# The last two tiles' products of v and gates are dealt out between the last group's maxima, and the first head's row goes ahead of v

## The chip, the cores and the metric

The kernel runs on one core of a Trainium2 chip. The metric is the device time of one execution in microseconds (us); several executions are timed and their median is compared. One execution is also taken by the hardware profiler; it has a time of its own.

The engines are named as in the profile: PE is the matrix engine (PEld its weight loads), DVE the vector engine, ACT the scalar engine, POOL the general engine, SP the engine that issues most DMAs. A name with q behind it (SPq, ACTq) is the DMA queue that the engine feeds.

## The reference, cut to what matters

One layer over a sequence of 2048 tokens with width 1024. The input projection gives q, k and v (8 heads of 64) and u and g (512 columns each):

```
proj = einsum('bsd,de->bse', rms_norm(x), w_in)       # 1024 -> 3*512 + 2*512
q, k = per-head rms_norm(q), rms_norm(k)
a    = dilated_attention(q, k, v)     # branches (window, dilation) = (128,1), (512,4), (2048,16)
m    = spatial_gating(gelu(u), gelu(g), ...)
x    = x + concat(rms_norm(a), rms_norm(m)) @ w_out
x    = x + square(relu(rms_norm(x) @ w_ff1)) @ w_ff2
```

Each branch is a causal window softmax over the keys with the same residue, and the three branches are added with the weights of their softmax denominators. The kernel needs one number for each query and head that is at least as large as any of its scores, so that the exponentials don't overflow; it takes the largest score over the three branches. All products are done in a 32-bit form in which a number is held as a high and a low part: a product is three matmuls (high by high, low by high, high by low).

## The kernel before, in words

**Sweep 1** (`sweep1`, L340 to L613) goes over 16 tiles of 128 tokens. For each tile t it projects q, k and v (columns c = 0, 1, 2), 24 matmuls of 128x512 each (`gemm3`; 8 blocks of the width by three products). q and k are normed; v is split and stored (`v_d`, one store a tile, L572). Behind the product of the next tile, `behind(t, q, k, step)` does the rest of a tile in three steps: step 0 transposes q and k, splits them and stores them (`qt_d`, `kt_d`); step 1 (`max1`) computes the scores of the first branch again and takes their maxima; step 2 folds these into the tile's row of maxima. After every four tiles (a group G) the maxima of the second branch follow (`max4`), dealt out as `late4` over the next four tiles; `fold4` merges them and `store_m` stores the row to `mx_d`.

A call of `maxima` takes the units two by two, called a *pair* here: two matmuls into one bank `ps_sc` (L452) and two DVE maxima that read them (L456). There are two such banks. `max1` has four pairs for a tile (operand `qz`, 128 rows). `max4` has two pairs for a head and group (operand `qhi`, 64 rows, every fourth element of `kring` and `qhi`), 16 pairs for the 8 heads.

At the end of sweep 1 there is no next tile to stand between: `behind(15, 0)`, then the gates' products g of tiles 14 and 15 (24 matmuls each; their weights are loaded and split from t = 15 on into the places of q's weights: DMA `graw`, ACT `zh`, DVE `zl`), then `behind(15, 1)` (four pairs), `behind(15, 2)`, and `rest`, the second branch's maxima of the last group. Each g is copied by ACT into one buffer `ge` (L589) and stored to `ge_d` (ACT queue, L590).

**Attention** (`attention`, from L616) goes over the 8 heads. `prepare(h)` issues the loads on SP: `qh` (high part of q, loaded twice, once into rows 0 to 63 and once into rows 64 to 127), `ks` (high and low part of k), `q2` (low part of q) and `k2` (high part of k), and on the ACT queue `m14`, the stored maxima (L646). `load_v(1)` loads v for the first branch (`v1`), `load_v(4)` those for the two others. The maxima of the third branch are taken here: `group(r0)` (L662) does four matmuls `ps_mx<-ks,qh`; after four groups, DVE merges the result with `m14`, PE transposes it, and DVE's `nm` (minus the maximum) is sent by a DMA, here called the *row*, into row 64 of `q2`, so that the score matmul subtracts it by itself. The row has to be there before the second score matmul of the head can run.

For a head there are 20 jobs of scores, exponentials and products with v (`ps_as` L74, then `ps_o`): jobs 0 to 7 for the first branch, then four times two jobs for the second branch and one for the third. The groups of the next head are laid at the jobs named in `MXAT`. For head 0 there is no head before it, so sweep 1's last pairs are put around its groups: the pairs of heads 0 and 1 before `attention`, those of heads 2 and 3 ahead of its groups, those of heads 4 to 7 behind the row.

**What sets the order.** A scheduler places the instructions of an engine, except those given by `InOrder` or by a name in `en.pinned`: these stay in program order on their engine. All of attention is in order on every engine (its lines read L74 in the profile, the line of the helper). DMA issues of SP and of ACT are in order within their engine, and an issue waits for the data it sends, for its buffer, and for the DMA that had its completion counter before it.

Of the kernel before, what the change touches and what calls it, by code (L numbers as in the profile page):

```python
# [8 lines left out]
F32 = mybir.dt.float32  # L9
F32R = mybir.dt.float32r  # L10
AF = mybir.ActivationFunctionType
# [5 lines left out]
P = 128  # L17
S = 2048
D = 1024
H = 8  # L20
HD = 64
AW = H * HD
GW = 512
# [3 lines left out]
NT = S // P  # L27
KD = D // P
VW = 2 * HD + 2
# [5 lines left out]

MXAT = (5, 8, 11, 14)
V1AT, V4AT = 12, 4
# [10 lines left out]
LATE_H = 4  # L48
RH = 4
SPL = 0  # L50
LAB = True
WP1 = ()
BYP = ((0, 0),)
# [6 lines left out]
PIN2, PINM, PINE = 12, (), ()  # L60
PSB, MXB, HS0 = 4, 1, 0


# [40 lines left out]
def tile_hybrid_block(  # L104
# [20 lines left out]
    nc = tc.nc  # L125
# [180 lines left out]
    wg = {}  # L306
# [33 lines left out]
    def sweep1():  # L340
        if True:
# [7 lines left out]
            zh, zl = wg_tiles()  # L349
            wh = [zh] + [[wp.tile([P, AW], F32R, name=f"wh{c}_{k}") for k in range(KD)] for c in (1, 2)]  # L350
            wl = [zl] + [[wp.tile([P, AW], F32R, name=f"wl{c}_{k}") for k in range(KD)] for c in (1, 2)]
            vts = []
# [54 lines left out]
            def transposed(qn, gain, hi, lo):  # L407
                pt = pst.tile([P, 4, P], F32, tag="tr", name="ps_tr")
                for j in range(4):
                    nc.tensor.transpose(pt[:, j, :], qn[:, j * P : (j + 1) * P], ident)  # L410
# [33 lines left out]

            order = [nc.tensor, nc.vector]

            def maxima(m, units):

                for i in range(0, len(units), 2):
                    ps = pss.tile([P, 2, 256], F32, tag="sc", name="ps_sc")  # L450
                    for j, (qv, kv, mk, col) in enumerate(units[i : i + 2]):
                        order[0].matmul(ps[:, j, : mk.shape[1]], qv, kv, start=True, stop=True)  # L452
                    for j, (qv, kv, mk, col) in enumerate(units[i : i + 2]):
                        n = mk.shape[1]
                        jk = sp.tile([P, 256], F32, tag="jk", name="jk", bufs=1)
                        order[1].tensor_tensor_reduce(  # L456
                            jk[:, :n], ps[:, j, :n], mk, 1.0, -3e38, ALU.add, ALU.max, accum_out=m[:, col : col + 1]
                        )
# [84 lines left out]
            def late4(t, n):  # L543
# [6 lines left out]
                if tg == 3:  # L550
                    fold4(G, m4s.pop(G))
                    store_m(G, range(H))

            last = None
            gsrc = w_in[:, 3 * AW + GW : 3 * AW + 2 * GW]
            for t in range(NT):
                en.pinned = PINT if t < 1 else ()
                if 0 < t < NT - 1:
                    xs[t + 1] = load_x_t(xp, pst, t + 1, newton=True)
                _, xh, xl, r = xs[t]  # L560
                ns = []
                for c in range(3):
                    ps = psm.tile([P, AW], F32, tag="mm", name="ps_mm")
                    gemm3(ps, [(xh[:, k, :], xl[:, k, :], wh[c][k], wl[c][k]) for k in range(KD)], (t, c) in BYP)
                    if (t, c) == (0, X1AT):
                        xs[1] = load_x_t(xp, pst, 1, newton=True, xt=x_1)
                    if c < 2:
                        ns.append(normed(ps, r))
                    else:
                        vt = vts[t % 2]  # L570
                        split_sb(vt[:, :, 0:HD], vt[:, :, HD + 2 : VW], ps.rearrange("p (h d) -> p h d", d=HD), r)
                        nc.sync.dma_start(v_d[:, t * P : (t + 1) * P, :].rearrange("h t c -> t h c"), f32(vt))  # L572
                    if last is not None:
# [8 lines left out]
                late4(t, 2)  # L582
            behind(NT - 1, *last, 0)
            for t in (NT - 2, NT - 1):
                _, xh, xl, r = xs[t]
                ps = psm.tile([P, AW], F32, tag="mm", name="ps_mm")
                gemm3(ps, [(xh[:, k, :], xl[:, k, :], wg["h"][k], wg["l"][k]) for k in range(KD)])
                ge = sp.tile([P, GW], F32, tag="sq", name="ge", bufs=1)
                nc.scalar.activation(ge, ps, AF.Copy, scale=r)  # L589
                nc.scalar.dma_start(ge_d[t - NT + 2], ge)  # L590
            behind(NT - 1, *last, 1)
            behind(NT - 1, *last, 2)
            G = NT // 4 - 1
            nc.vector.memset(m4s[G], -3e38)

            def rest(heads):
                max4(G, m4s[G], qhis[G], heads)
                fold4(G, m4s[G])
                store_m(G, heads)

            rest(range(0, 2))
            st.close()
# [13 lines left out]
    def attention(finish, xnp, xs, tpe, wu):  # L616
        with ExitStack() as st:
# [12 lines left out]
            def prepare(h):  # L630
# [30 lines left out]

                def group(r0, psm=psm, queue=sy):  # L662
                    ps = psm.tile([P, 4, P], F32, tag="mx", name="ps_mx")
                    for j in range(4):
                        s = r0 + j
                        pe.matmul(ps[:, j, :], qh[0:HD, s * P : (s + 1) * P], ks[0:HD, s::16], start=True, stop=True)

                    def row():
                        nm = tp.tile([P, P], F32R, tag="nm", name="nm", bufs=1)[:16]
                        dve.tensor_scalar(nm, ps[:16, 0, :], -1.0, None, ALU.mult)  # L670
                        queue.dma_start(f32(q2[HD : HD + 1, :]), f32(nm))

# [826 lines left out]
```

## Time and profile before

| | us |
|---|---|
| timed executions | 2424.43, 2413.07, 2421.35 |
| their median | 2421.35 |
| the profiled execution's own time | 2430.62 |
| its span | 2428.9 |
| mean granted PE clock in it | 0.963 |
| sweep 1's last tiles to the first score of head 0 | about 330 to 410 in the span |
| attention | about 410 to 700 in the span |

A timeline row has the start in us from the span's start, the duration, the engine, the line, the operation with out<-in, the shape and count, and in brackets the idle time of the engine ahead of it and what ended it. Matmuls overlap in the pipe, so the distance of two starts is what one costs, not its duration. A row of windows has, for each stretch of time, the busy time and number of instructions of each engine, then the granted PE clock (1.00 is full, 0.50 half), the share of DMA time and the GB/s moved. The page's line of PE clock holds it in tenths for 40 slices of 60.7 us.

### The profile page before, as it was taken

The numbers are of one execution on the slowest core, as the hardware profiler recorded it, in microseconds if no ns is written. First come the engines' busy times: TensorE is split into PE (matmuls) and PEld (weight loads), VectorE is DVE, ScalarE is ACT, GpSimd is POOL, SyncE is SP. The second block draws the span as 40 slices with busy tenths as digits, with TensorE's granted clock in tenths as the row PEclk, the third lists the DMA queues.
The fourth block names the chain that finished last, engine by engine and source line by source line (L and its number), as shares of the span: only waits on it lengthen the run. The fifth ranks groups of instructions, "written<-read, shape, count | busy, mean of one in ns | idle before, by whom it ended". The sixth has DMA issues, their size and how long they took to land. (4 is left out here: it accounts for less than half of the span.)

```text
span 2428.9 us, 31778 instructions
## 1 busy us (share of the span) xinstructions
PE 2346.2 (97%) x11292; PEld 1962.2 (81%) x11292; DVE 1462.1 (60%) x2940; ACT 972.6 (40%) x1584; POOL 861.2 (35%) x691
## 2 busy tenths in 40 slices
PE   8999998999997999998989998999999999999999
PEld 7877776999995888777778886788878888888887
DVE  6666676556555656665875558655547565565542
ACT  5323323566663222223535555555543232222321
POOL 1101103555551222221566776677752001221210
PEclk9999997789888999998999999999999999999999
DMA  5445358576833333333666456655559665575652
GB/s 189 86 88 109 71 113 177 166 191 175 230 114 94 96 100 94 87 95 122 207 201 180 148 155 200 188 151 152 156 180 332 211 204 187 185 241 179 192 172 78
DMA packets 432302, 382.35 MB, mean 157 GB/s; under 512 B 89704, under 2 KB 358632, under 8 KB 427528
## 3 DMA queue, kind: packets, MB, share of 16 engines
q1 hardware_dynamic: 415408, 377.68, 53.4%
q10 hardware_dynamic: 16736, 2.65, 0.7%
q8 instruction: 89, 1.46, 0.2%
q14 instruction: 69, 0.57, 0.1%
HBM read 259.80 MB, written 120.39 MB: 157 GB/s over the span
## 5 line engine op out<-in xcount | busy, mean ns | idle before, releaser
L1298 PE MATMUL ps_f<-hop,wop 128*128 128x512 f32 x2688 | 620.3, 393 | 13.4 <-ACT hop L188 3.2
L1420 PE MATMUL ps_f<-split 128*128 128x512 f32 x2688 | 611.0, 390 | 2.8 <-ACT c L1285 2.8
L1298 PEld LDWEIGHTS ps_f<-hop,wop 128*128 128x128 f32 x2688 | 507.4, 189 | 124.6 <-ACT hop L188 5.0
L1420 PEld LDWEIGHTS ps_f<-split 128*128 128x128 f32 x2688 | 505.7, 188 | 108.0 <-ACT c L1285 3.2
L1210 POOL TENSOR_TENSOR as<-w1r 128x512 f32<-128x512 f32 x160 | 211.7, 1331 | 167.1 <-DVE wop L189 147.0
L1430 DVE TENSOR_TENSOR acc<-acc,ps_f 128x512 f32<-128x512 f32 x192 | 124.5, 683 | 212.1 <-PE ps_f L1420 212.0
L188 ACT ACTIVATE split<-sr 128x1024 fp32r<-128x1024 f32 x112 | 118.4, 1059 | 333.2 <-PE ps_f L1420 324.8
L1210 POOL TENSOR_TENSOR raw<-raw 128x1024 f32<-128x1024 f32 x40 | 101.0, 2532 | 420.8 <-DMA raw<-in_w_ff_dram 353.0
L1210 POOL TENSOR_TENSOR c<-c 128x512 f32<-128x512 f32 x160 | 233.5, 1482 | 45.8 <-ACT c L1286 45.8
L74 POOL TENSOR_TENSOR pl<-e,ph 128x512 fp32r<-128x512 f32 x144 | 175.2, 1229 | 145.4 <-ACT e L74 116.0
L189 DVE TENSOR_TENSOR wop<-as,wop 128x512 fp32r<-128x512 f32 x160 | 151.2, 945 | 88.3 <-ACT wop L188 85.6
L188 ACT ACTIVATE wop<-as 128x512 fp32r<-128x512 f32 x160 | 100.5, 629 | 210.6 <-POOL as L1210 122.4
L74 DVE TENSOR_TENSOR ps_as<-ps_as,mk 128x512 f32<-128x512 f32 (+1 forms) x160 | 105.9, 664 | 123.1 <-PE ps_as L74 112.7
L189 DVE TENSOR_TENSOR split<-sr,split 128x1024 fp32r<-128x1024 f32 x112 | 157.1, 1404 | 17.1 <-ACT split L188 12.5
L74 PE MATMUL ps_o<-ph,v 128*64 128x128 f32 (+3 forms) x816 | 154.2, 276 | 1.8 <-ACT nacc L74 1.4
L74 PE MATMUL ps_as<-qh,ks 128*128 128x256 f32 (+1 forms) x384 | 143.2, 378 | 0.0
L74 ACT ACTIVATE ph<-ps_as 128x512 fp32r<-128x512 f32 (+1 forms) x160 | 92.3, 577 | 125.3 <-DVE ps_as L74 125.0
L74 PE MATMUL ps_as<-q,k 65*128 65x256 f32 (+1 forms) x384 | 139.0, 371 | 0.0
L456 DVE CUSTOM_DVE_ANT_0 jk<-ps_sc,mk 128x256 f32<-128x256 f32 (+1 forms) x232 | 92.5, 399 | 45.8 <-PE ps_sc L452 39.7
L526 POOL CAST qz<-qhi 64x512 fp32r<-64x512 f32 x32 | 19.6, 613 | 274.4 <-ACT qhi L414 273.4
L74 PEld LDWEIGHTS ps_o<-ph,v 128*65 128x65 f32 (+1 forms) x816 | 114.7, 158 | 2.2 <-ACT nacc L74 1.6
L74 PEld LDWEIGHTS ps_as<-qh,ks 128*128 128x128 f32 x384 | 108.3, 282 | 2.9
(266 smaller groups left out, 4109.2 us busy)
## 6 DMA issues: line engine op xcount, KB each, us to landing
s_d<-c SPq DMA_DIRECT2D x224, 256.0 KB, 2.2
sr<-s_d SPq DMA_DIRECT2D x112, 512.0 KB, 3.6
raw<-in_w_ff_dram SPq DMA_DIRECT2D x96, 512.0 KB, 4.9
w1r<-in_w_ff_dram SPq DMA_DIRECT2D x128, 256.0 KB, 3.0
v<-v_d SPq DMA_DIRECT2D x24, 1040.0 KB, 12.3
xt<-in_x_dram SPq DMA_DIRECT2D x32, 512.0 KB, 4.0
raw<-h_d SPq DMA_DIRECT2D x28, 512.0 KB, 5.5
v_d<-vt SPq DMA_DIRECT2D x16, 520.0 KB, 7.9
```

The costliest lines, as they stand in the source:

```text
L74: return self.tc.keep_in_program_order(op(*args, **kwargs))
L188: en.scalar.activation(dst_hi, raw, AF.Copy)
L189: (en.gpsimd if on_pool else en.vector).tensor_tensor(dst_lo, raw, f32(dst_hi), ALU.subtract)
L456: order[1].tensor_tensor_reduce(jk[:, :n], ps[:, j, :n], mk, 1.0, -3e38, ALU.add, ALU.max, accum_out=m[:, col : col + 1])
L526: nc.gpsimd.tensor_copy(qz[rows, hh], f32(qhis[G][rows, :, cols]))
L1210: nc.gpsimd.tensor_tensor(dst, a, b, op)
L1298: nc.tensor.matmul(ps[bank], a[:, k, :], b[k], start=first and k == n == 0, stop=(k == 3 and n == 2), skip_group_check=True,)
L1420: nc.tensor.matmul(ps, s[a][:, k, :], t[b][:, k % 2, :], start=k == m == 0, stop=k == NH - 1 and m == 2)
L1430: nc.vector.tensor_tensor(c, c, ps, op)
```

## The change

The change has five parts.

1. The v products of tiles 14 and 15 and the g products of both, 96 matmuls, no longer stand in blocks. They become a list of *fillers*, taken one by one in order (v14, v15, g14, g15): 12 behind the k product of tile 15, 8 and 12 ahead of steps 0 and 1 of `behind(15)`, and 3 between the matmuls and the DVE maxima of each pair from then on. From tile 15's last step on, PE is pinned to this order.
2. All 16 pairs of the last group run in sweep 1 (heads 0 and 1, then 2 to 7), none around head 0's groups. `finish` only closes pools.
3. Head 0's row goes out on the SP queue like those of the other heads, and its `load_v(1)` is issued behind the row and no longer with the head's other loads.
4. `prepare` loads `qh` twice first and `ks` as one DMA of 128 rows; a group's matmul takes 128 rows (both parts of k) in place of 64.
5. `MXAT` is (7, 9, 12, 14) in place of (5, 8, 11, 14). The weights of v are allotted ahead of those of k.

```diff
-MXAT = (5, 8, 11, 14)
+MXAT = (7, 9, 12, 14)
+FILL, FILL0, FILL1, FILL2 = 3, 12, 8, 12
...
+            fillers = []
+            def fill(n):
+                for f in [fillers.pop(0) for _ in range(min(n, len(fillers)))]:
+                    f()
             def maxima(m, units):
...
                         order[0].matmul(ps[:, j, : mk.shape[1]], qv, kv, start=True, stop=True)
+                    fill(FILL)
                     for j, (qv, kv, mk, col) in enumerate(units[i : i + 2]):
...
+            def in_parts(t, w, store):
+                _, xh, xl, r = xs[t]
+                got = {}
+                def part(k, n):
+                    if k == n == 0:
+                        got["ps"] = psm.tile([P, AW], F32, tag="mm", name="ps_mm")
+                    a, b = ((xh, w[0]), (xh, w[1]), (xl, w[0]))[n]
+                    end = (k, n) == (KD - 1, 2)
+                    en.tensor.matmul(got["ps"], a[:, k, :], b[k], start=k == n == 0, stop=end)
+                    if end:
+                        store(t, got["ps"])
+                return [lambda k=k, n=n: part(k, n) for k in range(KD) for n in range(3)]
...
+                    elif t < NT - 2:
+                        store_v(t, project(t, c))
...
+                    if t == NT - 1 and c == 2:
+                        en.pinned, order[0] = ("tensor",), en.tensor
+                        for u in (NT - 2, NT - 1):
+                            fillers += in_parts(u, (wh[2], wl[2]), store_v)
+                        for u in (NT - 2, NT - 1):
+                            fillers += in_parts(u, (wg["h"], wg["l"]), store_g)
+                        fill(FILL0)
                     if last is not None:
                         behind(t - 1, *last, c)
...
-            behind(NT - 1, *last, 0)
-            for t in (NT - 2, NT - 1):
...
-                gemm3(ps, [(xh[:, k, :], xl[:, k, :], wg["h"][k], wg["l"][k]) for k in range(KD)])
...
-            behind(NT - 1, *last, 1)
-            behind(NT - 1, *last, 2)
+            for step in range(3):
+                fill((FILL1, FILL2, 0)[step])
+                behind(NT - 1, *last, step)
             G = NT // 4 - 1
             nc.vector.memset(m4s[G], -3e38)
-            def rest(heads):
+            for heads in (range(0, 2), range(2, H)):
                 max4(G, m4s[G], qhis[G], heads)
                 fold4(G, m4s[G])
                 store_m(G, heads)
-            rest(range(0, 2))
+            fill(len(fillers))
+            en.pinned = ()
             st.close()
             def finish(pe, dve):
-                order[:] = pe, dve
                 yield lambda pool: load_x_t(pool, pst, 0, nxt=1)
-                rest(range(2, RH))
                 yield
-                rest(range(RH, H))
                 late.close()
...
-                sy.dma_start(f32(qh[0:HD, :]), qt_d[h, 0:HD, :])
-                sy.dma_start(f32(ks[0:HD, :]), kt_d[h, 0:HD, :])
-                sy.dma_start(f32(ks[HD:P, :]), kt_d[h, HD:P, :])
+                for rows in (slice(0, HD), slice(HD, P)):
+                    sy.dma_start(f32(qh[rows, :]), qt_d[h, 0:HD, :])
+                sy.dma_start(f32(ks), kt_d[h])
                 sy.dma_start(f32(q2[0:HD, :]), qt_d[h, HD:P, :])
-                sy.dma_start(f32(qh[HD:P, :]), qt_d[h, 0:HD, :])
...
-                        pe.matmul(ps[:, j, :], qh[0:HD, s * P : (s + 1) * P], ks[0:HD, s::16], start=True, stop=True)
+                        pe.matmul(ps[:, j, :], qh[:, s * P : (s + 1) * P], ks[:, s::16], start=True, stop=True)
...
-                        queue.dma_start(f32(q2[HD : HD + 1, :]), f32(nm))
+                        sy.dma_start(f32(q2[HD : HD + 1, :]), f32(nm))
...
             T, group, load_v = prepare(0)
-            load_v(1)
...
-                for reduce in [group(r0, psx if r0 else psm, nc.scalar) for r0 in range(0, 16, 4)]:
+                for reduce in [group(r0, psx if r0 else psm) for r0 in range(0, 16, 4)]:
                     reduce()
                 due(True)
                 due(True)
+            load_v(1)
```

**PE at the end of sweep 1, before.** `zh` and `zl` are the gates' weights, `xh` and `xl` the tile, `kring` the keys, `ps_tr<-ident,m` the transposes of a fold. These rows run from the last g product to the first scores of head 0.

```order
L226 MATMUL ps_mm<-zl_3542,xh 128x512
L227 MATMUL ps_mm<-zh_3538,xl 128x512
L452 MATMUL ps_sc<-kring,qz 128x256 x8
L452 MATMUL ps_sc<-kring,qhi 128x256 x2
L478 MATMUL ps_tr<-ident,m_3818 8x128
L452 MATMUL ps_sc<-kring,qhi 128x256 x6
L500 MATMUL ps_tr<-ident,m_3850 8x128 x4
L74 MATMUL ps_sc<-kring,qhi 128x256 x8
L74 MATMUL ps_tr<-ident,m_3850 8x128 x4
L74 MATMUL ps_mx<-ks,qh 128x128 x16
L74 MATMUL ps_mx<-ident,m_3915 16x128
L74 MATMUL ps_sc<-kring,qhi 128x256 x16
```

The same place of the changed program, its last rows ahead of the first score:

```order
L458 MATMUL ps_sc<-kring,qhi 128x256 x2
L74 MATMUL ps_mm<-zh_3510,xl 128x512
L74 MATMUL ps_mm<-zh_3510,xh 128x512
L74 MATMUL ps_mm<-zl_3514,xh 128x512
L458 MATMUL ps_sc<-kring,qhi 128x256 x2
L74 MATMUL ps_mm<-zh_3510,xl 128x512
L458 MATMUL ps_sc<-kring,qhi 128x256 x4
L507 MATMUL ps_tr<-ident,m_3803 8x128 x4
L74 MATMUL ps_mx<-ks,qh 128x128 x16
L74 MATMUL ps_mx<-ident,m_4005 16x128
L74 MATMUL ps_as<-qh,ks 128x256
L74 MATMUL ps_as<-q_3995,k_3996 128x256
```

The 16 pairs of the last group (32 matmuls `ps_sc<-kring,qhi`) stood bare behind the products, 8 of them (16 matmuls) behind head 0's transpose. They now have three products behind each of the first 13 and one behind the 14th; two are bare, and between the transpose and the first score nothing is left.

**SP's queue for head 0, before**, from its first load on (`q_3904` and `k_3905` are q2 and k2, `v_3916` is v1; the loads of head 1 follow):

```order
L74 DMA qh<-qt_d 64x2048
L74 DMA ks<-kt_d 64x2048 x2
L74 DMA q_3904<-qt_d 64x2048
L74 DMA qh<-qt_d 64x2048
L74 DMA k_3905<-kt_d 64x2048
L74 DMA v_3916<-v_d 128x16x130
L74 DMA qh<-qt_d 64x2048
L74 DMA ks<-kt_d 64x2048 x2
```

And of the changed program, where `q_3995` and `k_3996` are q2 and k2, `v_4068` is v1:

```order
L571 DMA v_d<-vt_191 128x8x130
L74 DMA qh<-qt_d 64x2048 x2
L74 DMA ks<-kt_d 128x2048
L74 DMA q_3995<-qt_d 64x2048
L74 DMA k_3996<-kt_d 64x2048
L74 DMA qh<-qt_d 64x2048
L74 DMA q_3995<-nm 1x16x128
L74 DMA v_4068<-v_d 128x16x130
```

The store of v of tile 15 now stands directly ahead of head 0's loads (it stood ahead of ten stores of q and k). The row (`<-nm`) is on this queue, behind k2 and the first load of head 1 and ahead of v1.

**ACT at the same place, before**, where `ge` is the copy of a gate product, `m_3913` is m14 of head 0 and `q_3904<-nm` the row:

```order
L589 ACTIVATE ge<-ps_mm,xss 128x512
L506 DMA mx_d<-mrow 2x512
L590 DMA ge_d<-ge 128x512
L589 ACTIVATE ge<-ps_mm,xss 128x512
L590 DMA ge_d<-ge 128x512
L646 DMA m_3913<-mx_d 128x16
```

And of the changed program, where `m_4003` is m14 of head 0:

```order
L513 DMA mx_d<-mrow 2x512
L575 ACTIVATE ge<-ps_mm,xss 128x512
L576 DMA ge_d<-ge 128x512
L575 ACTIVATE ge<-ps_mm,xss 128x512
L576 DMA ge_d<-ge 128x512
L676 DMA m_4003<-mx_d 128x16
```

The order is nearly the same: head 0's m14 is issued behind the store of the second gate product in both. That product's last matmul stands ahead of all 20 bare pairs before, and behind 14 of the last group's 16 pairs now.

More of the change, by code (lines that the diff above doesn't have):

```diff
@@ L48 @@
 LATE_H = 4
-RH = 4
 SPL = 0
@@ L349, in sweep1 @@
             zh, zl = wg_tiles()
-            wh = [zh] + [[wp.tile([P, AW], F32R, name=f"wh{c}_{k}") for k in range(KD)] for c in (1, 2)]
-            wl = [zl] + [[wp.tile([P, AW], F32R, name=f"wl{c}_{k}") for k in range(KD)] for c in (1, 2)]
+            wh = [zh] + [[wp.tile([P, AW], F32R, name=f"wh{c}_{k}") for k in range(KD)] for c in (2, 1)][::-1]
+            wl = [zl] + [[wp.tile([P, AW], F32R, name=f"wl{c}_{k}") for k in range(KD)] for c in (2, 1)][::-1]
             vts = []
@@ L409, in transposed @@
                 for j in range(4):
-                    nc.tensor.transpose(pt[:, j, :], qn[:, j * P : (j + 1) * P], ident)
+                    order[0].transpose(pt[:, j, :], qn[:, j * P : (j + 1) * P], ident)
                 if gain is None:
@@ L552, in late4, with project, store_v, store_g @@
                     store_m(G, range(H))
+            def project(t, c):
+                _, xh, xl, r = xs[t]
+                ps = psm.tile([P, AW], F32, tag="mm", name="ps_mm")
+                gemm3(ps, [(xh[:, k, :], xl[:, k, :], wh[c][k], wl[c][k]) for k in range(KD)], (t, c) in BYP)
+                return ps
+            def store_v(t, ps):
+                vt = vts[t % 2]
+                r = xs[t][3]
+                split_sb(vt[:, :, 0:HD], vt[:, :, HD + 2 : VW], ps.rearrange("p (h d) -> p h d", d=HD), r)
+                nc.sync.dma_start(v_d[:, t * P : (t + 1) * P, :].rearrange("h t c -> t h c"), f32(vt))
+            def store_g(t, ps):
+                ge = sp.tile([P, GW], F32, tag="sq", name="ge", bufs=1)
+                nc.scalar.activation(ge, ps, AF.Copy, scale=xs[t][3])
+                nc.scalar.dma_start(ge_d[t - NT + 2], ge)
+            def in_parts(t, w, store):
+                _, xh, xl, r = xs[t]
+                got = {}
[8 more added lines that the diff above has]
+                return [lambda k=k, n=n: part(k, n) for k in range(KD) for n in range(3)]
             last = None
@@ L559, in sweep1 @@
                     xs[t + 1] = load_x_t(xp, pst, t + 1, newton=True)
-                _, xh, xl, r = xs[t]
                 ns = []
                 for c in range(3):
-                    ps = psm.tile([P, AW], F32, tag="mm", name="ps_mm")
-                    gemm3(ps, [(xh[:, k, :], xl[:, k, :], wh[c][k], wl[c][k]) for k in range(KD)], (t, c) in BYP)
+                    if c < 2:
+                        ns.append(normed(project(t, c), xs[t][3]))
+                    elif t < NT - 2:
+                        store_v(t, project(t, c))
                     if (t, c) == (0, X1AT):
                         xs[1] = load_x_t(xp, pst, 1, newton=True, xt=x_1)
[L567 to L572, printed above, removed]
+                    if t == NT - 1 and c == 2:
[5 more added lines that the diff above has]
+                        fill(FILL0)
                     if last is not None:
@@ L582, in sweep1 @@
                 late4(t, 2)
-            behind(NT - 1, *last, 0)
-            for t in (NT - 2, NT - 1):
-                _, xh, xl, r = xs[t]
-                ps = psm.tile([P, AW], F32, tag="mm", name="ps_mm")
-                gemm3(ps, [(xh[:, k, :], xl[:, k, :], wg["h"][k], wg["l"][k]) for k in range(KD)])
-                ge = sp.tile([P, GW], F32, tag="sq", name="ge", bufs=1)
-                nc.scalar.activation(ge, ps, AF.Copy, scale=r)
-                nc.scalar.dma_start(ge_d[t - NT + 2], ge)
-            behind(NT - 1, *last, 1)
-            behind(NT - 1, *last, 2)
+            for step in range(3):
+                fill((FILL1, FILL2, 0)[step])
+                behind(NT - 1, *last, step)
             G = NT // 4 - 1
             nc.vector.memset(m4s[G], -3e38)
-            def rest(heads):
+            for heads in (range(0, 2), range(2, H)):
                 max4(G, m4s[G], qhis[G], heads)
@@ L660, in prepare, with group @@
                 m16 = few(tp, 16, "m16", 2)
-                def group(r0, psm=psm, queue=sy):
+                def group(r0, psm=psm):
                     ps = psm.tile([P, 4, P], F32, tag="mx", name="ps_mx")
```

## The prediction, made before the changed kernel was timed

> **What bounds the kernel now.** I read the page's shares and clock first, then the stages around the change by windows, then the rows of single waits.
>
> ```profile
> PE 2346.2 (97%) x11292; PEld 1962.2 (81%) x11292; DVE 1462.1 (60%) x2940; ACT 972.6 (40%) x1584; POOL 861.2 (35%) x691
> ...
> PEclk9999997789888999998999999999999999999999
> ```
>
> PE is busy 97% of the span, so what counts is where it idles and where its clock is low. Of the 40 slices of 60.7 us, the 7th to 13th (364 to 789 us) are the long low ones. The change lies at their beginning. By windows around it:
>
> ```profile
> 329.70:351.20 21.50, 21.50 (x95) 16.67 (x94) 15.87 (x57) 6.55 (x12) 1.25 (x2) 1.00 0.37 87
> 351.20:376.00 24.80, 23.20 (x103) 17.24 (x102) 14.00 (x49) 8.25 (x11) 5.93 (x6) 1.00 0.42 94
> 376.00:391.90 15.90, 10.80 (x35) 6.06 (x33) 11.54 (x50) 1.78 (x2) 1.28 (x2) 0.63 1.11 195
> 391.90:400.60 8.70, 3.64 (x16) 3.45 (x16) 4.71 (x34) 2.17 (x3) 1.80 (x1) 0.50 0.67 155
> 400.60:410.20 9.60, 7.69 (x21) 4.72 (x22) 7.20 (x33) 0.00 (x0) 0.00 (x0) 0.50 1.02 226
> 410.20:414.50 4.30, 4.30 (x21) 4.30 (x21) 3.50 (x5) 2.26 (x5) 1.03 (x1) 0.52 1.06 223
> ```
>
> Up to 376 PE is full (44.7 of 46.3 us). From 376 to 410.2 it is busy for 22.1 of 34.2 us, most of that at half clock. The rows tell why:
>
> ```profile
> 375.76 0.39 PE L227 MATMUL ps_mm<-zh,xl 128*128 128x512 f32 x1
> 375.99 0.63 PE L452 MATMUL ps_sc<-kring,qz 128*128 128x256 f32 x4
> 377.38 0.50 PE L452 MATMUL ps_sc<-kring,qz 128*128 128x256 f32 x2 [0.76 <-DVE m L456]
> 378.42 0.51 PE L452 MATMUL ps_sc<-kring,qz 128*128 128x256 f32 x2 [0.54 <-DVE m L456]
> ...
> 391.90 3.64 PE L74 MATMUL ps_mx<-ks,qh 64*128 64x128 f32 x16 [0.86 <-issue]
> 400.65 0.38 PE L74 MATMUL ps_mx<-ident,m 128*16 128x128 f32 x1 [5.11 <-DVE m L74]
> ...
> 410.20 0.55 PE L74 MATMUL ps_as<-qh,ks 128*128 128x256 f32 x1
> ...
> 414.52 0.28 PE L74 MATMUL ps_o<-ph,v 128*65 128x256 f32 x1
> ```
>
> A bare pair costs 1.04 us (377.38 to 378.42), and PE waits for DVE's maxima in it. Head 0's groups end at 395.5, then PE idles 5.1 us for the merged maxima; behind the transpose the last 8 pairs fill the time up to the first score at 410.2. So the seam is a chain of DVE and DMA, and only a shorter chain gains.
>
> **The change: what dealing out saves.** What a pair costs with three products behind it stands in the trace of before, since such pairs are there already in the blocks:
>
> ```profile
> 331.36 0.48 PE L452 MATMUL ps_sc<-kring,qz 128*128 128x256 f32 x2
> ...
> 332.38 0.51 PE L452 MATMUL ps_sc<-kring,qz 128*128 128x256 f32 x2
> ...
> 364.35 0.83 PE L452 MATMUL ps_sc<-kring,qhi 64*128 64x256 f32 x2
> 365.11 0.50 PE L227 MATMUL ps_mm<-zh,xl 128*128 128x512 f32 x1
> ...
> 366.00 0.83 PE L452 MATMUL ps_sc<-kring,qhi 64*128 64x256 f32 x2
> ```
>
> A first-branch pair with three products takes 1.02 us (331.36 to 332.38): its products are free, as a bare one takes 1.04. A strided second-branch pair with three takes 1.65 us (364.35 to 366.00), of which the pair alone holds PE 0.76 (to 365.11). Apart they cost 1.04 + 3 x 0.23 = 1.73 (0.23 is 375.76 to 375.99). So dealing out saves about 0.7 us for each of tile 15's four first-branch pairs and 0.08 for each strided one: 2.8 + 14 x 0.08 = 3.9 us in all. Strided pairs nearly fill PE by themselves.
>
> **The new order, laid out from the start of v14's products in the trace of before (329.7).** v14 goes away from the first window and takes 24 x 0.23 = 5.5 us with it, so k15 ends at 351.2 - 5.5 = 345.7. Tile 14's four first-branch pairs now stand without products: 4 x 1.04 = 4.2, and between their maxima DVE holds the splits of the gates' weights. Before, one such wait cost 1.6 us:
>
> ```profile
> 357.49 0.50 PE L452 MATMUL ps_sc<-kring,qz 128*128 128x256 f32 x2 [1.60 <-DVE m L456]
> ```
>
> I take 2 for it (between 0, if the weights come earlier with the rest, and 4, since the splits' loads keep their pace while the pairs come 5.5 us sooner): 351.9. Then 12 products (2.8), four strided pairs with 12 (6.6), 20 products and 12 transposes (4.6 + 1.3, from 0.11 for a transpose), four first-branch pairs with 12 (4.1): 371.3. The last group: 13 x 1.65 + 1.0 puts the last g15 product at 393.8; two bare pairs and the folds (2.1 + 1.5) end at 397.4.
>
> Now head 0's chain, in which each link has its row:
>
> ```profile
> 386.68 0.35 ACTq L590 DMA_DIRECT2D ge_d<-ge  x1
> 392.37 0.69 ACT L589 ACTIVATE ge<-ps_mm,xss 128x512 f32<-128x512 f32 x1 [9.25 <-DMA ge_d<-ge]
> 393.08 0.35 ACTq L590 DMA_DIRECT2D ge_d<-ge  x1
> 393.53 1.06 ACTq L646 DMA_DIRECT2D m<-mx_d  x1
> ...
> 400.42 0.17 DVE L74 TENSOR_TENSOR m<-m,m 128x16 f32<-128x16 f32 x1 [3.73 <-DMA m<-mx_d]
> ...
> 401.38 0.61 ACTq L671 DMA_DIRECT2D q<-nm  x1
> ```
>
> m14 was issued at 393.53, behind the second copy of `ge`, which waited for the first store to land. The merge waited for m14 until 400.42, and the row went out 0.96 us later. In the new order the second copy waits for the product instead: 393.8 + 1.16 (392.37 to 393.53) = 395.0 for m14's issue, 1.5 us later than before, and 401.9 for the merge. The groups compete: `ks` is issued when the store of v15 has landed, and that store waits for v15's split, which DVE does behind the 8th of the 16 pairs (about 385).
>
> ```profile
> v<-v_d SPq DMA_DIRECT2D x24, 1040.0 KB, 12.3
> ...
> v_d<-vt SPq DMA_DIRECT2D x16, 520.0 KB, 7.9
> ...
> ks<-kt_d SPq DMA_DIRECT2D x16, 512.0 KB, 6.9
> ...
> q<-nm SPq DMA_DIRECT2D x7, 8.0 KB, 1.8
> ...
> q<-nm ACTq DMA_DIRECT2D x1, 8.0 KB, 7.6
> ```
>
> 385 + 7.9 + 6.9 = 399.8, plus 3.6 for the groups at half clock (391.90's row): 403.4. That is later than m14, so the transpose is at 403.4 and the row is issued at about 404.3 (before 401.4). It lands 1.8 us later if it goes like the later heads' and 7.6 if like head 0's, whose queue was full; k2 and a load of head 1 are ahead of it, so I take 4: first score at 408.3, against 410.2. The pairs that covered this time are gone, and PE idles there instead; the cover is paid back by the path. **Term one: -1.9 us**, between -4.4 and +1.7.
>
> v1 is issued at about 404.9. In before it went out at 401.28 and its first use at 414.52 shows no wait.
>
> ```profile
> 400.64 0.60 SPq L74 DMA_DIRECT2D k<-kt_d  x1
> 401.28 0.59 SPq L74 DMA_DIRECT2D v<-v_d  x1
> ```
>
> k2 (issued when the second gate store has landed: 395 + 5.7, the time from 386.68 to 392.37, so about 400.7, as before), 512 KB for head 1 and v1's 1040 KB make 2.06 MB, at the 226 GB/s of the window 400.6 to 410.2 that is 9.1 us: v1 is there at about 410 to 412. Its first use is 4.3 us behind the first score (410.20 to 414.52), at 412.6. **Term two: 0**, with 4.6 us to lose if v1 takes the median of 12.3 (417.2 against 412.6). The single DMA for `ks` and the reordered `qh` move the same bytes: 0.
>
> **The clock in attention, where the wider groups and MXAT act.** This is the large unknown. The same PE work of a head runs at full or at half clock:
>
> ```profile
> 503.00:506.50 3.50, 3.50 (x23) 3.50 (x23) 1.48 (x8) 2.58 (x5) 0.03 (x1) 1.00 1.06 348
> 506.50:509.90 3.40, 3.40 (x22) 3.23 (x21) 3.06 (x11) 2.91 (x5) 2.54 (x2) 1.00 0.99 412
> 509.90:530.40 20.50, 20.50 (x115) 20.27 (x116) 8.44 (x20) 9.16 (x17) 8.09 (x7) 0.50 0.35 85
> 530.40:537.20 6.80, 6.80 (x64) 6.62 (x64) 6.05 (x8) 4.80 (x11) 5.28 (x5) 1.00 1.05 224
> ...
> 506.58 0.69 PE L74 MATMUL ps_mx<-ks,qh 64*128 64x128 f32 x4
> ```
>
> The half-clock stretch of 20.5 us does 115 matmuls; at the 9.4 per us of 530.4 to 537.2 they would take 12.2, so one such stretch costs about 8 us. The drop comes behind 506.5 to 509.9, in which a group of 64 rows stands ahead of short score matmuls. [...] I find no reason for a sign: **term three: 0**, one stretch of 8 us either way.
>
> **The sum.** -1.9 + 0 + 0 against the profiled execution's 2430.62 gives 2428.7. That execution is 9 us above the median of the timed ones (2421.35), about one half-clock stretch; on the median's footing the forecast is 2419.5.
>
> **Rivals.**
> - *The wider groups keep the clock.* For it: the drop at 509.9 with PE fully busy. If two of the stretches of 8 us go, 2419.5 - 16 = 2403.5. Against: the short strided matmuls behind the group stay as they are. [...]
> - *Nothing covers head 0's row, and v comes late* (slower). The first products with v wait for v1 to 417.2 (+2.7 against 414.5); the idle time from 398 to 417 puts the first head at half clock, and moved groups add two more half-clock stretches, 16 us: 2421.4 + 2.7 + 16 = 2440. It decides when v1 takes more than 7.7 us from its issue (412.6 - 404.9) and the groups at jobs 7 and 9 fall in a window that drops. For it: 12.3 us is the median of v's loads. Against: the DMA engines are idle around 400 in before, and no head but the first sees the seam.
> - *The dealing out doesn't happen as meant*, because PE waits for DVE between fillers: then 0.08 us a pair becomes nothing and the fillers cost their 0.23 each; the seam is +2, 2423. Inside the forecast's neighbourhood.
>
> **How the numbers follow.** A measurement of this kernel can tell about 0.5% (12 us) from no change. Forecast 2419.5, with 2412 to 2428 as its own range: chance 0.55. Wider groups keep the clock: 0.25. Slower: 0.15. No effect in the seam: 0.05. Faster by over 0.5% is below 2409.2: nearly all of the first rival and a little of the forecast, 0.27. Slower by over 0.5% is above 2433.5: 0.13, most of the second rival. The rest, 0.60, is within. The range from 2402 to 2433 takes in the first rival's value and stops ahead of the second's.
>
> **What would show it right or wrong.** Strided pairs with products should start 1.6 to 1.7 us apart; if they come at 1.1, the seam gains 8 us more. The last g product should end near 394, m14 be issued near 395, the transpose stand at 402 to 404 behind an idle stretch of some us, the row's issue near 404 and the first score near 408. The first `ps_o<-ph,v` should show no wait for v. In attention I look at the granted clock from 410 to 700: before it is low in stretches of 14 to 20 us, and the number of these decides between forecast, first and second rival. I am wrong if the first score comes before 404 or after 412, or if the clock of attention moves by more than one such stretch.

## The result, and the profile after

The changed kernel took 2405.38 us (median of 5 runs, 2403.24 to 2409.50), the kernel before 2419.91 in the same comparison (5 runs, 2413.07 to 2424.43): a ratio of 0.994, 95% interval 0.9922 to 0.9958. It is faster by 14.5 us, 0.6%, which is small but clear of the noise. Run again later beside 32 runs of before, it gave 0.9955 (0.9939 to 0.9972). The forecast was 2419.5 with a range of 2402 to 2433; the time lies in the range, near its low end and near the first rival's value of 2403.5. It lies outside the forecast's own range, 2412 to 2428. The profiled execution's own time is 2405.38, its span 2403.7.

The page of the changed kernel, the same two lines as of before: busy time by engine, and the granted PE clock in 40 slices (of 60.1 us here).

```profile
PE 2323.3 (97%) x11288; PEld 1943.5 (81%) x11288; DVE 1455.7 (61%) x2939; ACT 971.2 (40%) x1584; POOL 861.8 (36%) x691
...
PEclk9999998999998999999999999999999999999999
```

Of the 7th to 13th slice, six stood below 9 in before (7 7 8 9 8 8 8); now only the 7th and the 13th do. PE is busy for 22.9 us less with only four matmuls less, so nearly the same matmuls took less time.

Windows of the changed kernel at the same times as in the prediction:

```profile
329.70:351.20 21.50, 18.09 (x76) 13.30 (x75) 17.87 (x71) 8.13 (x15) 1.22 (x2) 0.93 0.36 98
351.20:376.00 24.80, 24.80 (x98) 17.92 (x97) 15.07 (x57) 5.67 (x7) 4.55 (x6) 0.92 0.59 90
376.00:391.90 15.90, 15.90 (x52) 9.92 (x52) 9.62 (x39) 2.42 (x4) 2.72 (x2) 1.00 0.80 133
391.90:400.60 8.70, 6.38 (x19) 3.37 (x18) 5.18 (x21) 2.17 (x3) 1.80 (x1) 0.74 0.93 254
400.60:410.20 9.60, 4.24 (x18) 3.79 (x18) 3.99 (x34) 0.00 (x0) 0.00 (x0) 0.50 0.82 178
410.20:414.50 4.30, 3.74 (x17) 3.77 (x18) 2.20 (x4) 1.99 (x5) 0.75 (x1) 0.50 1.19 286
```

From 376 to 392 PE is now full at full clock, where it was busy for 10.8 us. From 400.6 to 410.2 it is nearly idle (4.24 us, most of that head 0's groups), where the last pairs stood before. PE's rows show the chain:

```profile
349.25 0.80 PE L458 MATMUL ps_sc<-kring,qz 128*128 128x256 f32 x2 [3.17 <-DVE m L463]
...
375.57 0.83 PE L458 MATMUL ps_sc<-kring,qhi 64*128 64x256 f32 x2
...
377.23 0.83 PE L458 MATMUL ps_sc<-kring,qhi 64*128 64x256 f32 x2
...
394.95 0.50 PE L74 MATMUL ps_mm<-zh,xl 128*128 128x512 f32 x1
...
400.65 3.65 PE L74 MATMUL ps_mx<-ks,qh 128*128 128x128 f32 x16 [2.02 <-DMA ks<-kt_d]
405.57 0.38 PE L74 MATMUL ps_mx<-ident,m 128*16 128x128 f32 x1 [1.27 <-DVE m L74]
...
410.76 0.55 PE L74 MATMUL ps_as<-q,k 65*128 65x256 f32 x1 [4.60 <-DMA q<-nm]
...
414.95 0.41 PE L74 MATMUL ps_o<-ph,v 128*65 128x256 f32 x1
```

The first product with v starts at 414.95; in before it started at 414.52. So the seam, where most of the edit lies, gains nothing in these traces. PE now waits for `ks`, then for DVE to take and merge the maxima of head 0's groups, then 4.6 us for the row.

The time is gained behind it. The last product of attention with v stands at 718.7 us in before and at 695.9 now: attention, from first to last product with v, takes 281.0 us in place of 304.2. What follows it takes 1707.7 us in place of 1710.2. Attention's windows of before, then of the changed kernel:

```profile
414.00:450.00 36.00, 35.70 (x233) 34.34 (x233) 18.28 (x55) 21.91 (x41) 21.08 (x18) 0.81 0.61 160
450.00:490.00 40.00, 39.89 (x271) 38.90 (x270) 22.79 (x61) 23.78 (x44) 21.71 (x18) 0.79 0.66 178
490.00:530.00 40.00, 40.00 (x264) 39.13 (x263) 22.50 (x60) 24.43 (x46) 21.71 (x18) 0.75 0.68 178
...
650.00:690.00 40.00, 39.52 (x252) 38.87 (x252) 21.50 (x53) 22.97 (x44) 19.16 (x17) 0.70 0.58 192
```

```profile
414.00:450.00 36.00, 36.00 (x276) 35.89 (x276) 22.41 (x62) 25.27 (x49) 24.02 (x21) 0.96 0.67 187
450.00:490.00 40.00, 39.40 (x314) 39.29 (x313) 25.58 (x65) 29.12 (x55) 27.85 (x23) 1.00 0.76 218
490.00:530.00 40.00, 40.00 (x294) 40.00 (x293) 24.46 (x70) 25.59 (x50) 24.04 (x21) 0.87 0.66 188
...
650.00:690.00 40.00, 37.63 (x280) 36.97 (x280) 26.94 (x38) 30.15 (x57) 24.10 (x19) 0.91 0.36 121
```

PE is full in both, but with 0.79 in place of 1.00 it gets 271 matmuls done in 40 us and not 314. Summed from the trace's record of the granted clock, attention has 92 us of half clock in before and 26 us now. The profiled execution of before is 10.7 us above its median, so the two spans differ by 25.2 us where the medians differ by 14.5; which part of the 25.2 is chance one trace cannot say. The mean granted clock of that execution, 0.963, is low: the median of 32 later executions of before is 0.968.

### The profile page after: what moved, and what is told of

It is laid out like the page before. It is cut to its first block, busy times and chain, and to the rows that moved or that the text cites. A ratio compares the mean times of both kernels' runs of the same rounds, so it can differ in the third digit from the quotient of the medians.

```text
span 2403.7 us, 31746 instructions
## 1 busy us (share of the span) xinstructions
PE 2323.3 (97%) x11288; PEld 1943.5 (81%) x11288; DVE 1455.7 (61%) x2939; ACT 971.2 (40%) x1584; POOL 861.8 (36%) x691
## 5 line engine op out<-in xcount | busy, mean ns | idle before, releaser
L74 PE MATMUL ps_o<-ph,v 128*64 128x128 f32 (+3 forms) x816 | 140.3, 259 | 1.4 <-ACT nacc L74 1.4
L74 PE MATMUL ps_as<-qh,ks 128*128 128x256 f32 (+1 forms) x384 | 137.3, 363 | 0.0
L463 DVE CUSTOM_DVE_ANT_0 jk<-ps_sc,mk 128x256 f32<-128x256 f32 (+1 forms) x256 | 102.7, 401 | 53.6 <-PE ps_sc L458 47.8
L74 PEld LDWEIGHTS ps_as<-q,k 65*128 65x128 f32 x384 | 108.4, 282 | 4.9 <-issue 4.9
L189 DVE TENSOR_TENSOR split<-raw,split 128x1024 fp32r<-128x1024 f32 x56 | 75.9, 1358 | 54.5 <-ACT split L188 52.2
```

What stands on the lines that cost most here:

```text
L74: return self.tc.keep_in_program_order(op(*args, **kwargs))
L189: (en.gpsimd if on_pool else en.vector).tensor_tensor(dst_lo, raw, f32(dst_hi), ALU.subtract)
L463: order[1].tensor_tensor_reduce(jk[:, :n], ps[:, j, :n], mk, 1.0, -3e38, ALU.add, ALU.max, accum_out=m[:, col : col + 1])
```

## The experiments

Three theories were put against one another. **R**: what grants PE its full or half clock (called the clock gate here) counts operand rows, so groups of 128 rows hold the clock. **M**: the new places in `MXAT` do it. **S**: the new order of the seam does it. After the first runs a fourth took over, **P**: the wide groups hold the clock, but they need all of `ks` and `qh`, so they gain only where they stand late enough.

All times are medians in us. The ratio is to runs of before on the same chip, whose medians were 2423.90 (beside after_64, after_mxold, rows_only and mxat_only), 2421.06 (beside rows_mxat, seam_only and the two padded kernels) and 2423.45 (beside seam_clean, blocks, after_again and best); it is not the quotient of the two medians, and differs from that by up to 0.0016. "Half clock" and "attention" are from the profiled execution, first to last product with v, and so is "waits of groups", PE's idle time ahead of `ps_mx<-ks,qh` from 416 to 690. These come from one execution each. Its mean clock is up to 0.005 away from the median of the kernel's executions, which over the whole span is an estimated 24 us of half clock, so small differences in that column mean little.

| run | what it has | time | ratio (95%) | half clock | attention | waits of groups |
|---|---|---|---|---|---|---|
| before | | 2419.91 | 1 | 92 | 304.2 | 0.0 |
| after | parts 1 to 5 | 2405.38 | 0.994 (0.9922 to 0.9958) | 26 | 281.0 | 2.5 |
| after_again | the same | 2412.87 | 0.9955 (0.9939 to 0.9972) | 31 | 283.2 | 3.3 |
| after_64 | groups of 64 rows | 2437.65 | 1.0056 (1.0037 to 1.0075) | 99 | 307.7 | 1.7 |
| after_mxold | old MXAT | 2431.60 | 1.0029 (1.0015 to 1.0044) | 36 | 303.8 | 18.7 |
| rows_only | part 4 alone | 2431.79 | 1.0044 (1.0027 to 1.0062) | 42 | 305.4 | 18.6 |
| mxat_only | MXAT alone | 2433.08 | 1.0030 (1.0015 to 1.0044) | 100 | 306.6 | 0.0 |
| rows_mxat | part 4 and MXAT | 2414.33 | 0.9977 (0.9965 to 0.9988) | 52 | 290.8 | 5.1 |
| seam_only | parts 1 to 3, new loads | 2445.23 | 1.0116 (1.0097 to 1.0134) | 51 | 314.1 | 17.0 |
| seam_clean | parts 1 to 3 alone | 2426.44 | 1.0018 (1.0004 to 1.0033) | 73 | 301.8 | 1.6 |
| blocks | after, not dealt out | 2413.90 | 0.9961 (0.9947 to 0.9975) | 10 | 277.5 | 2.5 |
| before_pad | before, q2 and k2 padded | 2408.06 | 0.9956 (0.9944 to 0.9967) | 3 | 282.6 | 0.0 |
| after_pad | after, padded | 2405.14 | 0.9945 (0.9930 to 0.9961) | 10 | 278.3 | 3.9 |
| best | seam, padded, old groups | 2411.76 | 0.9958 (0.9943 to 0.9973) | 11 | 285.9 | 1.3 |

### One piece taken out of the change

after_64 gives the groups 64 operand rows again:

```diff
-pe.matmul(ps[:, j, :], qh[:, s * P : (s + 1) * P], ks[:, s::16], start=True, stop=True)
+pe.matmul(ps[:, j, :], qh[0:HD, s * P : (s + 1) * P], ks[0:HD, s::16], start=True, stop=True)
```

> The changed kernel with groups of 64 operand rows again (the low part of k is left out of the group's products, as before the change); all else as changed. Theory R (the clock gate counts operand rows, the wide groups hold it): most of the gain goes, 2414 to 2420 us, with 70 to 100 us of half clock between 410 and 700 us of the span where the changed kernel has 30. Theory M (the places in MXAT do it) and theory S (the seam's new order does it): no change, 2403 to 2408 us and about 30 us of half clock.

The gain is gone, and the half clock is back (99 us): R, and against M and S. But the kernel is slower than before by 0.56%, which none of the three expected. Two runs below add up to most of it: the new places without wide groups cost 0.30% (mxat_only), and the seam 0.18% (seam_clean).

after_mxold puts the old places back:

```diff
-MXAT = (7, 9, 12, 14)
+MXAT = (5, 8, 11, 14)
```

> The changed kernel with MXAT (5, 8, 11, 14) again. Theory R: no loss, 2402 to 2409 us. Theory M: the gain goes, 2414 to 2420 us, and the half clock in attention is back at 70 us or more. Theory S: no change.

The gain is gone here too, yet only 36 us are at half clock. Neither R nor M fits. What PE waited for from 416 to 690, by the view of waits (time in all, times, longest), says why, after_mxold first and then the changed kernel:

```profile
PE ps_mx L74 <- DMA ks<-kt_d: 10.7, 4, 5.3
PE ps_mx L74 <- issue: 7.9, 3, 3.5
```

```profile
PE ps_mx L74 <- DMA ks<-kt_d: 1.9, 1, 1.9
PE ps_o L74 <- ACT nacc L74: 1.4, 1, 1.4
PE ps_o L74 <- POOL pl L74: 1.0, 2, 0.6
PE ps_mx L74 <- issue: 0.6, 1, 0.6
```

At job 5 the groups come before their loads: 18.6 us of waits over the heads, against 2.5 at job 7. A group of 64 rows needs only the first halves of `qh` and `ks`, which the kernel before issued first.

### One piece alone

rows_only is before with the new loads and the wide groups; mxat_only is before with the new places.

```diff
-                sy.dma_start(f32(ks[0:HD, :]), kt_d[h, 0:HD, :])
-                sy.dma_start(f32(ks[HD:P, :]), kt_d[h, HD:P, :])
+                sy.dma_start(f32(ks), kt_d[h])
...
+pe.matmul(ps[:, j, :], qh[:, s * P : (s + 1) * P], ks[:, s::16], start=True, stop=True)
```

> The kernel before with the new loads of qh and ks and groups of 128 operand rows, and nothing else of the change. Theory R: most of the gain is there, 2405 to 2411 us against 2420, with half clock in attention of 50 us or less. Theories M and S: 2417 to 2423 us and half clock as before (97 us in the profiled execution).

> The kernel before with MXAT (7, 9, 12, 14), and nothing else of the change. Theory M: 2405 to 2411 us. Theories R and S: 2416 to 2424 us, since the groups keep 64 rows and the seam its order.

rows_only more than halves the half clock (92 to 42 us) and is still slower than before, since the groups wait for 18.6 us. Its row of the groups, with the idle time ahead of them at the end, and that of mxat_only:

```profile
L74 PE MATMUL ps_mx<-ks,qh 128*128 128x128 f32 x112 | 18.9, 303 | 18.6 <-DMA ks<-kt_d 13.2 <-issue 5.4
```

```profile
L74 PE MATMUL ps_mx<-ks,qh 64*128 64x128 f32 x112 | 21.6, 326 | 0.0
```

mxat_only gains nothing and is slower by 0.3%, which no theory expected: the places alone have no wait to remove and 100 us of half clock (the median clock of its 12 executions is 0.9615, that of the 30 of before 0.9675). M falls. Each piece alone loses: rows_only by 18.6 us of waits, of which later places leave 5.1 (rows_mxat), and mxat_only by the clock, whose 100 us of half clock are 52 with wide groups at the same places (rows_mxat).

### The two halves of the change

rows_mxat is before with part 4 and the new MXAT; seam_only is the change with the old groups and MXAT, but with the new loads; seam_clean is that with the old loads too. The other half of part 5, the order in which the weights are allotted, stays with the two runs of the seam.

> The kernel before with the new loads, groups of 128 rows and MXAT (7, 9, 12, 14): parts 4 and 5, without the seam (parts 1 to 3). What the runs so far suggest (theory P: wide groups hold the clock but wait for ks at job 5, so parts 4 and 5 gain only together): about 14 to 20 us faster than before, with under 45 us of half clock in attention and under 6 us of waits for ks. Rival S (the seam's new order is needed for it): within 5 us of before.

> The changed kernel with groups of 64 rows and MXAT (5, 8, 11, 14): parts 1 to 3 (and the new order of loads). Theory P: within 6 us of before, first product with v within 3 us of before's 414.5, half clock in attention 80 to 110 us. Rival S: 8 us or more faster than before.

> Parts 1 to 3 of the change alone: the fillers, all pairs in sweep 1, the row on SP and v1 behind it; loads, groups of 64 rows and MXAT as before. Theory P (the gain is in attention, by wide groups with room for their loads): no gain, 2416 to 2428 us against 2421, first product with v at 414 to 417 us, half clock in attention 80 to 110 us, no wait for ks. Theory S (the seam gains): 8 us or more faster.

Parts 4 and 5 together gain 0.23% without the seam, less than P's 14 to 20 us: in its trace half clock fell to 52 us, not below 45, and head 0's groups, which need both halves of `ks` here and stand where before's did, waited 6.4 us for it. The seam alone (seam_clean) is 0.18% slower, with the first product with v at 415.2: S falls. Its half clock, 73 us, is a little below the 80 to 110 expected. seam_only missed its expectation by far: with the one DMA of 128 rows for `ks`, groups of 64 rows wait for it too (17.0 us), and the kernel is 1.2% slower. So the new loads cost 17 to 19 us of waits wherever the groups stay at job 5. Its half clock, 51 us, also lies below the 80 to 110 expected, though its groups are narrow: the groups' rows alone don't set the clock. That the 17.0 us of waits make this difference was not shown. seam_only and after_mxold differ in the rows of the groups alone, and there the narrow groups are slower by 0.9% (1.0116 against 1.0029).

The halves don't add up: -0.23% and +0.18% against -0.45 to -0.6% for the whole. Half clock differs between them (52 us in rows_mxat, 26 and 31 in the whole), though the heads' instructions stand in the same order. In the traces of before and of the changed kernel the granted clock changes on a grid of 3.41 us: its stretches last whole multiples of that, the half-clock ones in attention 3.4, 6.8, 10.2, 13.7, 17.1 or 20.5 us. Where a head falls on this grid may depend on the time at which attention starts; that this makes the difference was not tried, and it stays open.

### Rows alone

before_pad keeps the order, the loads and the groups of before. Only the second score matmul reads 128 rows in place of 65: `q2` and `k2` are kept for the whole of attention (the trace names both `k`), and rows 65 to 127 are zeros.

```diff
-                q2 = kq.tile([P, S], F32R, tag="q2", name="q2", bufs=1)[: HD + 1]
...
-                    k2s.append(kq.tile([P, S], F32R, tag="k2", name="k2", bufs=1)[: HD + 1])
+                    for two in (k2s, q2s):
+                        two.append(kq.tile([P, S], F32R, tag=("k2", "q2")[two is q2s], name="k2", bufs=1))
+                        nc.gpsimd.memset(f32(two[h][HD:P, :]), 0.0)
                     nc.gpsimd.memset(f32(k2s[h][HD : HD + 1, :]), 1.0)
-                k2 = k2s[h % 2]
+                k2, q2 = k2s[h % 2], q2s[h % 2]
```

> The kernel before with q2 and k2 padded by zeros from 65 to 128 operand rows in the second score matmul; same columns, same order, same loads, no group changed. If the gate counts operand rows times columns, half clock in attention falls from 92 us to under 25 and the time by 10 us or more, without any wait for ks. If it counts columns or busy time alone, or if rows of zeros don't count, nothing changes: within 5 us of before and 80 to 110 us of half clock.

> The changed kernel with the same padding. If rows count: half clock in attention falls to under 10 us, and the time is 4 to 10 us below the changed kernel's, some 20 us below before's. If not: as the changed kernel, about 14 us below before.

This is R by itself: half clock 3 us in place of 92, 0.44% faster, from multiplying zeros. The clock says so in all executions: its median is 0.979 in the 5 of before_pad and 0.970 in the 17 of before beside them. The windows of before_pad:

```profile
450.00:490.00 40.00, 39.81 (x308) 38.71 (x307) 26.03 (x73) 27.10 (x51) 26.24 (x22) 1.00 0.77 199
490.00:530.00 40.00, 40.00 (x299) 38.90 (x298) 24.50 (x71) 27.27 (x52) 25.30 (x22) 1.00 0.76 198
...
650.00:690.00 40.00, 37.51 (x291) 36.88 (x291) 28.46 (x39) 30.18 (x57) 24.98 (x20) 1.00 0.37 127
```

PE was at least as busy in before's windows (39.9, 40.0 and 39.5 us) and had 0.79, 0.75 and 0.70. In the changed kernel the padding takes half clock from 26 to 10 us, but its time is the changed kernel's (0.9945 against 0.994 and 0.9955): the expected 4 to 10 us more did not come. In its profile head 0 starts later (418.2), with 5.4 us of waits for `ks` at the seam.

The clock is not the whole gain. A group of four matmuls also takes less time with 128 rows than with 64, both at full clock. These rows run from the matmul ahead of a group to the one behind it, in before and then in the changed kernel:

```profile
506.43 0.22 PE L74 MATMUL ps_o<-ph,v 128*64 128x128 f32 x1
506.58 0.69 PE L74 MATMUL ps_mx<-ks,qh 64*128 64x128 f32 x4
507.20 0.51 PE L74 MATMUL ps_as<-qh,ks 128*128 128x256 f32 x1
```

```profile
434.10 0.22 PE L74 MATMUL ps_o<-ph,v 128*64 128x128 f32 x1
434.16 0.64 PE L74 MATMUL ps_mx<-ks,qh 128*128 128x128 f32 x4
434.62 0.43 PE L74 MATMUL ps_as<-qh,ks 128*128 128x256 f32 x1
```

That is 0.77 us against 0.52. Over all groups at full clock and without a wait the mean is 0.79 us in before (23 groups) and 0.53 in the changed kernel (24), so for the 28 groups between first and last product with v an estimated 7 us. before_pad gives a price for the clock: 89 us less half clock with 21.6 us less attention. At that price the 66 us less of the changed kernel are an estimated 16 of its 23.2 us. With the 7 for the shorter groups, less 2.5 of waits, that makes about 21; the other 2 us are open. Why rows change the time of a group no run shows.

### Dealing out, and a version for the seam

blocks is the change with the 96 products in two blocks and bare pairs:

```diff
-FILL, FILL0, FILL1, FILL2 = 3, 12, 8, 12
+FILL, FILL0, FILL1, FILL2 = 0, 48, 0, 48
```

> The changed kernel with the 96 products in two blocks of 48 (behind k of tile 15, and ahead of step 1) and none between the pairs. By the rows of before a strided pair with three products costs 1.65 us, apart 1.73, so dealing out is worth about 4 us in all: first product with v 2 to 5 us later than in the changed kernel (417 to 420), the whole 0 to 6 us slower than the changed kernel. Rival (dealing out hides the products behind the maxima): 10 us or more slower.

> The changed kernel once more, beside the same runs of before as the others. 2402 to 2409 us, ratio 0.992 to 0.996; if the earlier ratio was that of one chip, it is nearer to 1.

The first product with v stands at 421.0, against 415.0 and 416.7 in the two traces of the changed kernel: dealing out saves 4.3 to 6.0 us at the seam, for an expected 2 to 5. In the whole it doesn't show: 2413.90 against 2412.87 beside the same runs of before. after_again missed its expected time (2412.87 for 2402 to 2409), but its ratio of 0.9955 is within what was expected.

best has the seam, the padding, the loads, groups and MXAT of before, and the second gate product's store on SP, behind head 0's `k2`, so that no load of head 0 waits for it:

```diff
-                nc.scalar.dma_start(ge_d[t - NT + 2], ge)
+                if t < NT - 1:
+                    nc.scalar.dma_start(ge_d[t - NT + 2], ge)
+                else:
+                    held.append(lambda: InOrder(tc, nc.sync).dma_start(ge_d[t - NT + 2], ge))
```

> The seam of the change (parts 1 to 3), the loads, 64-row groups and MXAT of before, q2 and k2 padded by zeros to 128 rows, and the store of the second gate product on SP behind head 0's k2, so that none of head 0's loads waits for that store. If rows count, half clock in attention is under 15 us with no wait for ks; the row lands by 407 and the first product with v stands at 409 to 412 us in place of 415. 2396 to 2404 us, faster than before and than the changed kernel. If the row's wait stays: as the padded kernel before, about 2408.

It is no better than the changed kernel. The row's wait went from 4.6 to 2.0 us, but the transpose stands at 407.24, behind a wait of 4.58 us for the maxima that DVE merges with m14 (issued at 395.98), and the first product with v stands at 415.05:

```profile
407.24 0.38 PE L74 MATMUL ps_mx<-ident,m 128*16 128x128 f32 x1 [4.58 <-DVE m L74]
409.94 0.55 PE L74 MATMUL ps_as<-k,k 128*128 128x256 f32 x1 [2.04 <-DMA k<-nm]
415.05 0.47 PE L74 MATMUL ps_o<-ph,v 128*65 128x256 f32 x1 [0.72 <-DMA v<-v_d]
```

The queues' rows, of SP first and then of ACT, show that q2, `qh`'s second half and k2 now go out from 395.04 on, around m14:

```profile
395.04 0.44 SPq L74 DMA_DIRECT2D k<-qt_d  x1
395.53 0.60 SPq L74 DMA_DIRECT2D qh<-qt_d  x1
396.17 0.59 SPq L74 DMA_DIRECT2D k<-kt_d  x1
407.34 0.33 SPq L74 DMA_DIRECT2D ge_d<-ge  x1
```

```profile
395.98 2.02 ACTq L682 DMA_DIRECT2D m<-mx_d  x2
```

A guess, which no run shows, is that the small load was slowed by the 1.5 MB issued around it. No version ran clearly faster than the change; the padding of before alone reaches the same.

## Why the prediction was right, and where it failed

The time lies in the range because the range was stretched to take in the first rival's 2403.5. The forecast itself, a gain of 1.9 us at the seam and nothing in attention, did not come, and neither did the outcome held most likely, a change within 0.5% (it is 0.6% here, and 0.45% when run again). By its own sign (the clock of attention moves by more than one stretch of 14 to 20 us) the forecast was wrong: half clock there went from 92 to 26 us.

**Dealing out.** Right: strided pairs with products start 1.66 us apart (375.57 to 377.23), as forecast from before's 1.65, and blocks shows 4 to 6 us for a forecast 3.9.

**The path to the last gate product.** Forecast 393.8, measured 395.2 (394.95 and the 0.23 us that one product costs). The stall behind tile 14's pairs was 3.17 us for an estimated 2.

**Head 0's chain (term one, -1.9 us).** The mechanism was right and the sum off by 2: the links came as laid out (`ks` landing 400.65 for 399.8, the groups' end 404.3 for 403.4, row issued 406.29 for 404.3), and two were left out or short: DVE's maxima and merge behind head 0's last group (1.27 us of wait) and the row's landing, 4.5 us after its issue for an estimated 4. The first product with v moved by +0.4. (The term's lower bound doesn't follow from the figures shown: with the row landing in 1.8 us, 404.3 + 1.8 - 410.2 is -4.1, not -4.4.)

**v1 (term two, 0).** Right: the first product with v shows no wait, 4.2 us behind the row's arrival.

**The clock in attention (term three, 0).** Wrong, and here is most of the gain. The forecast found no reason for a sign and gave the wide groups a chance of 0.25 as a rival. The price of a half-clock stretch was too high: by before_pad a stretch of 20.5 us costs an estimated 5 us (21.6 x 20.5 / 89), not 8.

In hindsight the sign could have been read off the trace of before. For each window of 3.41 us on the grid of the clock's changes I summed columns times operand rows over 128 of PE's matmuls, each spread over the time to the next one's start (over its own duration where PE idles behind it). In before, of 652 windows at full clock, the 21 that are followed by half clock are exactly those with the lowest sums: they reach up to 2929, and the others start at 2981. By columns alone the best limit puts 4 of the 652 wrong. The limit is fitted to these windows, and it is not sharp: in the changed kernel the best one (3088) puts 2 wrong, 4 by columns. before_pad decides against columns alone: with the same columns in the same order, and 128 rows in place of 65 in the second score matmul, half clock in attention is 3 us in place of 92. That the count goes exactly with the rows is not shown.

How busy PE is, as the profile counts it, does not tell the clock here: from 490 to 530 PE was busy for 40.00 us in both, and before had 0.75 and before_pad 1.00.

**The time of a group.** The forecast let groups of 128 rows cost what groups of 64 cost. They take 0.53 us in place of 0.79, an estimated 7 us in all.

**The place of the groups.** The forecast treated MXAT and the loads at no cost ("the same bytes: 0"). That step failed as well: moved loads cost 17 to 19 us of waits with groups at job 5, and MXAT's new places are what removes them. The two errors hide each other in the whole.

**The rivals.** The first came true in cause, with the wider groups working only together with MXAT. That its 2403.5 lies so near 2405.38 is in part luck: it took two stretches of 8 us, where the traces have 66 us less half clock, about three stretches at an estimated 5 us each, and another estimated 7 us from the groups' own time. The second's mechanism was half there: the row's wait is bare (4.6 us), v was in time, and moved groups alone add 0.3% (mxat_only). The third did not happen.

## What to carry to other kernels

Where PE is busy and yet at half clock, look at the operand rows: here zeros in rows 65 to 127 of one matmul's operands took half clock from 92 to 3 us and the time down by 0.44%. An edit that widens a matmul can also make it wait for more data (18.6 us in rows_only), so widen and move it later together, and test the pair before either alone. An order of work that hides products behind maxima gains little when the pairs nearly fill PE by themselves (a strided pair with three products takes 1.66 us here, and an estimated 1.73 apart).

## What the runs showed of the hardware

- The clock was higher with rows of zeros: half clock in attention went from 92 to 3 us with the operands of one matmul padded from 65 to 128 rows (before_pad).
- A group of four short matmuls cost PE 0.79 us with 64 operand rows (mean of 23 in before) and 0.53 with 128 (mean of 24 in the changed kernel), at full clock.
- A pair of strided matmuls (every fourth element) spanned 0.83 us at either clock: at 364.35 in before (full clock, shown in the prediction) and at 402.80 (half clock):

```profile
402.80 0.83 PE L74 MATMUL ps_sc<-kring,qhi 64*128 64x256 f32 x2 [0.52 <-DVE m L74]
```

- A DMA issue was held for 5.6 us by a DMA whose data it does not use. SP's rows in the changed kernel:

```profile
386.64 0.38 SPq L571 DMA_DIRECT2D v_d<-vt  x1
387.13 1.71 SPq L74 DMA_DIRECT2D qh<-qt_d  x2
394.45 0.33 SPq L74 DMA_DIRECT2D ks<-kt_d  x1
```

  `ks` of head 0 goes out 5.6 us behind the end of the issue ahead of it (387.13 + 1.71). Its data had been stored long before (the last stores of k were issued by 370.6); it waits on the completion counter that the store of v, issued at 386.64, used last, and the view of waits puts 5.6 us of SP's time down to that store. With the order of loads of before (best), `ks` went out at 388.14, 1.07 us behind the store of v (387.07).
